# A float32 decoder trunk on one core: how the last SwiGLU's last pair of blocks is turned

## The chip, the core and the metric

The kernel runs on one core of a Trainium2 chip as one launch. The metric is the time of that launch on the device, in microseconds, as the median of several runs. Before the change it is 1646.18 us over three runs, which lie between 1645.61 and 1646.3 us.

Five instruction queues work side by side on the core: PE (matrix products; PEld is its weight load), DVE (vector work), ACT (scalar work and copies), POOL (here mostly an issuer of accumulating DMAs) and SP (an issuer of DMAs). Each works through its own instructions strictly in order, and they wait for each other by semaphores. DMAs are issued from SP, POOL and ACT and are carried out by the core's 16 DMA engines.

## What is computed

Two layers, each a SwiGLU, a mixing block (windowed attention and a short convolution) and a second SwiGLU, then a final norm; one sequence of 512 tokens, width 1024, SwiGLU width 2816, all in float32:

```python
def swiglu(h, w_gate, w_up, w_down):
    return (jax.nn.silu(h @ w_gate) * (h @ w_up)) @ w_down

for l in range(DEPTH):
    x = x + 0.5 * swiglu(rms_norm(x, ffn1_norm[l]), ffn1_wg[l], ffn1_wu[l], ffn1_wd[l])
    ...
    x = x + 0.5 * swiglu(rms_norm(x, ffn2_norm[l]), ffn2_wg[l], ffn2_wu[l], ffn2_wd[l])
return rms_norm(x, final_norm)
```

The change is in the fourth and last SwiGLU, between its up and its down projection.

## The kernel before, in words

**Float32 by parts.** Every float32 operand is split in two parts, a rounded high part (an ACT cast, `wh` for weights) and the rest (a DVE subtraction, `wl`), both at line 223. A product is three matrix multiplications of parts. The weights stream from memory into `raw` buffers (line 206 issues them from SP; line 218 issues from POOL those that are added on top of a loaded buffer), are split, and are used once. Each weight pair is split up to two groups ahead of PE (`SPLIT_AHEAD`), and loaded four groups ahead of that (`LOAD_AHEAD`).

**Seven products for eight.** Large products are done in 2x2 blocks with seven products (`CHAINS`, `SHARES`). The seven steps use the operands b11, b21, t2, t3, t1, t4, b22 of the activations (`Seven.make`, lines 592 to 612, which also splits them) and the forms a11, a12, s2, s3, s1, a22, s4 of the weights. A DVE addition at line 262 or 247 makes s2 in place, and a POOL DMA (line 292 or 285, shown as `raw<-raw`) makes s4.

**The stages of a SwiGLU.** The width of 2816 is 11 blocks of 256. Stage `w` with number b makes blocks b and b+1 of the activations (`winograd2`); its results `ups` are four tiles of 128 tokens x 512 columns. The down projection needs them turned, so that columns lie on partitions. In the last SwiGLU (`LAST`) the pairs 1, 3, 5, 7 and 9 are made one after the other. Then stage `s`, number 1, is the first group of the down projection: it takes the pairs 1 and 3, in seven steps of two halves (`share`, line 836). Stage `e`, number 5, is the last group: it takes the pairs 5, 7 and 9, in seven steps of three parts, two from the pairs 5 and 7 (`ends[0]`) and one from pair 9 (`ends[1]`), and ends with the final norm (`Finale.last`, line 1404).

**Two ways to turn a pair.** (1) By DMA, class `Crossing` for the pairs 1 to 7: ACT lays the 16-bit halves of the float32 words apart (`lay_apart`, line 138), SP issues a DMA transpose, and ACT joins the halves again. Class `Tail` does the same for pair 9 of the inner SwiGLUs (the second and the third), with two DMA transposes for each 128 tokens, one for each half: `during(n)` is called after step n of the first group of the down projection, sends token tiles 0 and 1 at n = 1 and 2 and 3 at n = 2 (line 1190), and joins the first half again at n = 5 (`rejoin`, line 1202). (2) On PE, for pair 9 of the last SwiGLU: `turn` (line 1104) transposes 128x128 squares into PSUM, and ACT copies them out (line 1111). Its four calls stand in `pending`, and `between` of the last SwiGLU's stage `s` flushes two of them after step 1 and two after step 2 of the first group, eight PE transposes each time.

**What sets the order.** The kernel is written as a program of operations; a scheduling layer orders each engine's instructions by its own estimate of when they are ready. `tc.issue_after` forces one order. A buffer's next user waits for the last reader of the one before it. Each DMA also waits until the DMA that took its completion semaphore before it has landed (eight such semaphores are used for those of SP, eight for those of POOL).

Of the kernel before, what the change touches and what calls it, by code (L numbers as in the profile page):

```python
# [8 lines left out]
F32 = mybir.dt.float32  # L9
# [7 lines left out]
P = 128  # L17
D = 1024
S = 512
# [6 lines left out]
NT = S // P  # L26
# [46 lines left out]
def trunk_kernel(  # L73
# [23 lines left out]
    nc = tc.nc  # L97
# [837 lines left out]
    def ffn(norm, stages, after=None, late=None):  # L935

        acts = {}
# [100 lines left out]
        def winograd2(b, between=None):  # L1038


            name = f"{norm.i}_{b}"
            accs = {}
            gates = [g2(f"gate_{name}_{t}") for t in range(NT)]
            ups = [None] * NT
            kept = {}

            hasty = first and b == max(blocks)

            def keep(what, u, src):
                kept[what, u] = g2(f"{what}_{name}_{u}")  # L1050
                nc.scalar.copy(kept[what, u], src)

            for step, (acc, operand, start) in enumerate(CHAINS):
                norm.make(operand)
                xh, xl = norm.forms[operand]
                if start:
                    tag = {"x": "mm", "y": "sc", "w": "aux"}[acc]
                    accs[acc] = [psum(tag, [P, S], f"{acc}_{name}_{u}") for u in range(2)]
                for h in range(2):
                    _, wh, wl = take_split()  # L1060
                    stream(accs[acc], wh, wl, xh, xl, h, start)
                    for u in range(2):
                        out = accs[acc][u]
                        if h == 0:
                            continue
                        if step == 0:
                            keep("p1", u, out)
                        if step == 1:
                            nc.vector.tensor_add(gates[u], out, kept["p1", u])
                            nc.scalar.activation(gates[u], gates[u], AF.Silu)  # L1070
                        if step == 2:
                            keep("u2", u, out)
                        if step == 3:
# [12 lines left out]
                if hasty and step == 5:  # L1086
                    crossing.append(Crossing(b, name, ups, {1: (2, 3)}))
                    for t in range(2):
                        crossing[-1].send(t)
                if not first and step < 3:  # L1090
                    norm.make(CHAINS[step + 4][1])
                if between:
                    between(step)
            if b in blocks and not hasty:
                crossing.append(Crossing(b, name, ups, {0: (0, 1), 1: (2, 3)}))
            if b in blocks:
                return
            if b in tails:
                crossing.append(Tail(b, name, ups))
                return  # L1100
            if b in few:
                raws[b] = [form(f"raw_a{n}_{name}", F32, (P, 2, S)) for n in range(2)]

            def turn(c, tag="sc"):
                tp = psum(tag, [P, S], f"at_{name}_{c}")
                for t in range(NT):
                    nc.tensor.transpose(
                        tp[:, t * P : (t + 1) * P], ups[t][:, c * P : (c + 1) * P], ident
                    )
                if b in few:  # L1110
                    nc.scalar.copy(raws[b][c // 2][:, c % 2, :], tp)
                    return
                if b + c // 2 not in acts:
                    acts[b + c // 2] = [form(f"a{n}_{name}_{c}", shape=(P, 2, S)) for n in "hl"]
                hi, lo = acts[b + c // 2]
                split(hi[:, c % 2, :], lo[:, c % 2, :], tp)

            pending.extend(lambda *tag, c=c: turn(c, *tag) for c in range(NT))

        class Crossing:  # L1120

# [51 lines left out]
        class Tail:  # L1173
# [9 lines left out]
            def during(self, n):  # L1183

                if n == 1:
                    self.to = [form(f"turned{h}_{self.name}", U16, (P, NT, S)) for h in range(2)]
                for t in {1: (0, 1), 2: (2, 3)}.get(n, ()):
                    halves = lay_apart(self.ups[t], f"{self.name}_{t}")
                    for h in range(2):
                        nc.sync.dma_start_transpose(  # L1190
                            self.to[h][:, :, t * P : (t + 1) * P], halves[:, h, :]
                        )
                if n == 5:
                    self.whole = g8(f"raw_a_{self.name}", F32, (P, 2, 2, S))
                    self.rejoin(0)

            def rejoin(self, j):

# [29 lines left out]

        def turns(step):

            if step < 2:
                flush()
            if step == 2:
                flush(2, "mm")
            crossing[:] = [c for c in crossing if not c.step()]

        crossing = []
        sevens = [b for what, b in stages if what == "s"]
        blocks = [b + j for what, b in stages if what in "se" for j in (0, 2)]
        few = [b + 4 for what, b in stages if what == "e"]  # L1240
        tails = [b[0] for what, b in stages if what == "d" and len(b) == 2]
        raws = {}
        pending = []

        def flush(n=1, *tag):
            for _ in range(n):
                if pending:
                    pending.pop(0)(*tag)

        end = None  # L1250
        kept = {}
# [1 line left out]
        for i, (what, b) in enumerate(stages):  # L1253
# [22 lines left out]

# [41 lines left out]
            for c, acc in down(rhs, b == (0,) and not first, final):  # L1318
# [7 lines left out]
                flush()  # L1326
# [435 lines left out]
```

## Time and profile before

| | |
|---|---|
| median of three runs | 1646.18 us (1645.61 to 1646.3) |
| the profiled execution's own time | 1645.93 us |
| its span, first to last instruction | 1644.1 us |
| PE, DVE, ACT, POOL busy | 1633.7, 1376.6, 1107.4, 212.4 us |
| DMA, mean over the span | 186 GB/s |
| first group of the last down projection, on PE | 1539 to 1579 us |
| last group, up to the last product | 1579 to 1638 us |

The profile is one execution. A row of the chain of waits has a start and a length in us and what ran then. A row of instructions in order of time has a start, a length, the engine, the line of the kernel, what is written and read, and in brackets how long the engine was idle before it and what ended that. A row on a tile or a line has the shortest, middle and longest duration in ns. A row of windows has the stretch, then each engine's busy time in it, the granted clock of PE, the mean busy share of the 16 DMA engines (packets that overlap in one engine count twice, so that it can pass 1) and what they moved in GB/s.

### The profile page before, as it was taken

To read this page: it belongs to the slowest core of one execution; us is meant where nothing else is said; L and a number is where in the kernel's file an instruction comes from. 1 tells how busy PE (TensorE), PEld (TensorE's weight loads), DVE (VectorE), ACT (ScalarE), POOL (GpSimd) and SP (SyncE) were. 2 spreads that over 40 slices of the span, in tenths; PEclk is the share of its full clock that TensorE was granted. 3 is DMA by queue.
4 is the path that set the end of the run, shared out by engine and by line. 5 is a ranking of instruction groups with operands and counts; after the bars stand their busy time and mean duration, and the time that the engine had idled before them with its cause. 6 is when DMAs were issued, how large, how long until landed. Compare 5 with 4: busy or idle time off the path is not lost.

```text
span 1644.1 us, 22037 instructions
## 1 busy us (share of the span) xinstructions
PE 1633.7 (99%) x8076; PEld 1380.6 (84%) x8076; DVE 1376.6 (84%) x1812; ACT 1107.4 (67%) x1453; POOL 212.4 (13%) x188
## 2 busy tenths in 40 slices
PE   9999999999999999999999999999999999999998
PEld 7888889988898888888888888888888988888886
DVE  7987779988899977797998777989788998777997
ACT  6447776566567577777765777786565766777665
POOL 0011111100221111111011111110012111111121
PEclk9999999999999999999999999999999999999999
DMA  8379997741397689999866999997125967999992
GB/s 257 86 196 212 220 250 184 173 127 52 103 226 181 181 211 220 217 222 219 220 152 171 226 210 232 206 242 198 52 65 136 229 148 187 222 218 228 248 242 77
DMA packets 277280, 306.10 MB, mean 186 GB/s; under 512 B 93804, under 2 KB 162484, under 8 KB 277172
## 3 DMA queue, kind: packets, MB, share of 16 engines
q1 hardware_dynamic: 236580, 222.24, 46.9%
q0 software_dynamic: 39872, 81.80, 28.9%
q8 instruction: 63, 1.03, 0.2%
q10 hardware_dynamic: 720, 0.66, 0.1%
q14 instruction: 45, 0.37, 0.1%
HBM read 262.71 MB, written 2.10 MB: 161 GB/s over the span
## 4 chain that ended last, share of the span: by engine, by line
PE 94%; DVE 4%; ACT 1%; issue 1%; DMA 0%; SPq 0%; ACTq 0%; DVEq 0%
PE x L827 25%; PE y L827 13%; PE acc L321 8%; PE acc L322 8%; PE acc L324 8%; PE w L827 6%; PE x_s L827 5%; PE x_m L812 3%; PE y_s L827 3%; PE x_s L812 2%; PE w_s L827 2%; PE y_s L812 1%; PE y_m L812 1%; DVE wl L223 1%; PE acc L707 1%; PE x_e L827 1%
## 5 line engine op out<-in xcount | busy, mean ns | idle before, releaser
L223 ACT CAST wh<-raw 128x1024 fp32r<-128x1024 f32 (+1 forms) x491 | 511.1, 1044 | 367.0 <-PE x L827 91.9
L223 DVE TENSOR_TENSOR wl<-raw,wh 128x1024 fp32r<-128x1024 f32 (+1 forms) x491 | 594.6, 1218 | 176.7 <-ACT wh L223 175.6
L321 PE MATMUL acc<-xh,wh 128*128 128x512 f32 x424 | 165.8, 393 | 0.0
L322 PE MATMUL acc<-xl,wh 128*128 128x512 f32 x424 | 165.5, 390 | 0.0
L324 PE MATMUL acc<-xh,wl 128*128 128x512 f32 x416 | 162.3, 390 | 0.0
L218 POOL DMA_DIRECT2D raw<-in_ffn_wu_dram x39 | 48.7, 1248 | 393.9 <-DMA raw<-in_ffn_wu_dram 290.4
L322 PEld LDWEIGHTS acc<-xl,wh 128*128 128x128 f32 x424 | 79.7, 188 | 15.8 <-DVE xl L502 0.2
L321 PEld LDWEIGHTS acc<-xh,wh 128*128 128x128 f32 x424 | 79.8, 188 | 15.7
L324 PEld LDWEIGHTS acc<-xh,wl 128*128 128x128 f32 x416 | 78.1, 188 | 16.3
L218 POOL DMA_DIRECT2D raw<-in_ffn_wg_dram x39 | 48.2, 1262 | 228.5 <-DMA raw<-in_ffn_wu_dram 126.7
L218 POOL DMA_DIRECT2D raw<-in_ffn_wd_dram x34 | 41.0, 1207 | 251.7 <-DVE wl L223 64.1
L262 DVE TENSOR_TENSOR raw<-raw,raw 128x1024 f32<-128x1024 f32 x56 | 68.1, 1220 | 4.7 <-DMA raw<-in_ffn_wu_dram 3.1
L1158 ACT COPY raw_a<-turned 128x1024 uint16<-128x1024 uint16 x48 | 63.1, 1356 | 0.0
L827 PE MATMUL w<-wh,fb21h 128*128 128x512 f32 x152 | 59.2, 390 | 0.0
L827 PE MATMUL w<-wl,fb21h 128*128 128x512 f32 x152 | 59.2, 390 | 0.0
L827 PE MATMUL y<-wh,ft3h 128*128 128x512 f32 x152 | 59.2, 390 | 0.0
L827 PE MATMUL x<-wh,ft2h 128*128 128x512 f32 x152 | 59.2, 390 | 0.0
L827 PE MATMUL x<-wl,ft1h 128*128 128x512 f32 x152 | 59.2, 389 | 0.0
L827 PE MATMUL w<-wh,fb21l 128*128 128x512 f32 x152 | 59.2, 389 | 0.0
L827 PE MATMUL x<-wh,ft1l 128*128 128x512 f32 x152 | 59.2, 389 | 0.0
L827 PE MATMUL x<-wl,ft2h 128*128 128x512 f32 x152 | 59.2, 389 | 0.0
L827 PE MATMUL x<-wl,fb11h 128*128 128x512 f32 x152 | 59.2, 389 | 0.0
(607 smaller groups left out, 4624.3 us busy)
## 6 DMA issues: line engine op xcount, KB each, us to landing
raw<-in_ffn_wu_dram SPq DMA_DIRECT2D x126, 512.0 KB, 5.1
raw<-in_ffn_wd_dram SPq DMA_DIRECT2D x105, 512.0 KB, 5.9
raw<-in_ffn_wg_dram SPq DMA_DIRECT2D x86, 512.0 KB, 5.2
raw<-in_ffn_wu_dram POOLq DMA_DIRECT2D x39, 512.0 KB, 9.0
raw<-in_ffn_wg_dram POOLq DMA_DIRECT2D x39, 512.0 KB, 6.7
raw<-in_w_in_dram SPq DMA_DIRECT2D x36, 512.0 KB, 3.8
raw<-in_ffn_wd_dram POOLq DMA_DIRECT2D x34, 512.0 KB, 9.2
raw<-raw POOLq DMA_DIRECT2D x21, 512.0 KB, 7.0
```

The lines of the kernel that those rows point to most:

```text
L218: nc.gpsimd.dma_start(out=r, in_=rows_of(*more), accum_op=ALU.add)
L223: return nc.scalar.copy(hi, raw), eng.tensor_sub(lo, raw, f32(hi))
L262: nc.vector.tensor_add(a11, a11, s1)
L321: nc.tensor.matmul(acc, hi[:, k, :], rhs[k][0], start=k == first, stop=False)
L322: nc.tensor.matmul(acc, hi[:, k, :], rhs[k][1], start=False, stop=False)
L324: nc.tensor.matmul(acc, lo[:, k, :], rhs[k][0], start=False, stop=k == last)
L707: nc.tensor.matmul(opening[n], (lo if part == "w" else hi)[:, k, :], xl if part == "x" else xh, start=n not in begun, stop=k == KC - 1 and ...
L812: nc.tensor.matmul(accs[c // 2][:, c % 2, :], w[:, k, cols], x_[:, 2 * h + k, :], start=start and c % 2 == 0 and h + k + i == 0, stop=h + ...
L827: nc.tensor.matmul(accs[u], x_[:, 2 * h + k, tok], w[:, k, :], start=start and h + k + i == 0, stop=h + k == 2 and i == 2, skip_group_chec ...
L1158: nc.scalar.copy(words(raws[self.b][:, c, :]), self.to[:, :, c, :])
```

## The change

Pair 9 of the last SwiGLU becomes a `Tail`, as that of the inner ones is. The PE transposes, their PSUM tiles and `pending` with its `flush` go. After step 1 and step 2 of the first group `during` lays the halves apart and issues four DMA transposes each. After step 5 it joins the first half again, as in the inner ones, and after step 6, new and for the last SwiGLU alone, the second. `ends[1]` then reads the joined tile: its operand b11 is made after step 6 instead of step 4, and t2, which was made after step 6, is now made in the last group itself, before its second step. The two 16-bit tiles take two buffers of the pool `xf` in place of the two that held the copies, and the joined tile takes one of the pool `g8`.

```diff
-            if b in blocks:
-                return
             if b in tails:
                 crossing.append(Tail(b, name, ups))
-                return
-            if b in few:
-                raws[b] = [form(f"raw_a{n}_{name}", F32, (P, 2, S)) for n in range(2)]
-
-            def turn(c, tag="sc"):
-                tp = psum(tag, [P, S], f"at_{name}_{c}")
-                for t in range(NT):
-                    nc.tensor.transpose(
-                        tp[:, t * P : (t + 1) * P], ups[t][:, c * P : (c + 1) * P], ident
-                    )
-                if b in few:
-                    nc.scalar.copy(raws[b][c // 2][:, c % 2, :], tp)
-                    return
...
-            pending.extend(lambda *tag, c=c: turn(c, *tag) for c in range(NT))
...
                 if n == 5:
                     self.whole = g8(f"raw_a_{self.name}", F32, (P, 2, 2, S))
+                    raws[self.b] = [self.whole[:, j] for j in range(2)]
                     self.rejoin(0)
+                if n == 6 and after is None:
+                    self.rejoin(1)
...
-            if step < 2:
-                flush()
-            if step == 2:
-                flush(2, "mm")
             crossing[:] = [c for c in crossing if not c.step()]
...
-        few = [b + 4 for what, b in stages if what == "e"]
         tails = [b[0] for what, b in stages if what == "d" and len(b) == 2]
+        tails += [b + 4 for what, b in stages if what == "e"]
...
-                    for n, full in enumerate((lambda b=b: [raws[b + 4], raws[b + 6]], raws[b + 8]))
+                    for n, full in enumerate((lambda b=b: [raws[b + 4], raws[b + 6]], lambda b=b: raws[b + 8]))
                 ]
 
                 def between(step):
-                    if 0 < step < 3:
-                        flush(2, "mm")
-                    for at, n, operand in ((3, 0, "b11"), (4, 1, "b11"), (5, 0, "t2"), (6, 1, "t2")):
+                    for at, n, operand in ((3, 0, "b11"), (5, 0, "t2"), (6, 1, "b11")):
                         if step == at:
                             ends[n].make(operand)
```

As built, the scheduling layer moves these in the last 110 us, and nothing before. PE's order is the same but for the 16 transposes. On SP the eight DMA transposes and the first two loads of the last group come ahead of the two loads of the final norm's gain (line 1409), and these stand just before and just after the first of the two loads of form a22 of the first group; before, the gains came first of all and the loads of a22 stood between those of the last group. On ACT the four copies of line 138 stand around the casts of the first group's forms a12 and s2. On DVE the operands of pair 9 (t2's two subtractions among them) come later, t3 and the sum for t1 of the pairs 5 and 7 move from before to behind the third of the last group's s2 additions, and the low part of the first group's b22 comes one place earlier.

More of the change, by code (lines that the diff above doesn't have):

```diff
@@ L1095, in winograd2 @@
                 crossing.append(Crossing(b, name, ups, {0: (0, 1), 1: (2, 3)}))
-            if b in blocks:
-                return
             if b in tails:
                 crossing.append(Tail(b, name, ups))
-                return
-            if b in few:
-                raws[b] = [form(f"raw_a{n}_{name}", F32, (P, 2, S)) for n in range(2)]
-            def turn(c, tag="sc"):
-                tp = psum(tag, [P, S], f"at_{name}_{c}")
-                for t in range(NT):
-                    nc.tensor.transpose(
-                        tp[:, t * P : (t + 1) * P], ups[t][:, c * P : (c + 1) * P], ident
-                    )
-                if b in few:
-                    nc.scalar.copy(raws[b][c // 2][:, c % 2, :], tp)
-                    return
[L1113 to L1116, printed above, removed]
-            pending.extend(lambda *tag, c=c: turn(c, *tag) for c in range(NT))
         class Crossing:
@@ L1239, in ffn @@
         blocks = [b + j for what, b in stages if what in "se" for j in (0, 2)]
-        few = [b + 4 for what, b in stages if what == "e"]
         tails = [b[0] for what, b in stages if what == "d" and len(b) == 2]
+        tails += [b + 4 for what, b in stages if what == "e"]
         raws = {}
[L1243 to L1248, printed above, removed]
         end = None
@@ L1325, in ffn @@
                 )
-                flush()
                 if final and c == KC // 2:
```

## The prediction

> **What bounds the kernel now.** First the page: is any engine full, and which one carries the chain that ended last?
>
> ```profile
> span 1644.1 us, 22037 instructions
> ...
> PE 1633.7 (99%) x8076; PEld 1380.6 (84%) x8076; DVE 1376.6 (84%) x1812; ACT 1107.4 (67%) x1453; POOL 212.4 (13%) x188
> ...
> PE 94%; DVE 4%; ACT 1%; issue 1%; DMA 0%; SPq 0%; ACTq 0%; DVEq 0%
> ```
>
> PE is full and carries 94% of the chain, so work taken off PE is time, unless another engine then ends the waits. Second, the chain in the place of the change, from the first group of the last down projection into the last group.
>
> ```profile
> 1550.07 0.87 PE at L1107 x8
> ...
> 1556.40 0.87 PE at L1107 x8
> ...
> 1568.17 5.44 PE y_s L827 x24
> ...
> 1576.38 0.80 DVE wl L223
> ...
> 1586.38 0.60 DVE bias L1379
> ...
> 1589.31 4.83 PE x_e L827 x20
> ```
>
> The transposes are two pieces of the chain, 0.87 us each. But from 1576.38 to 1589.31 the chain runs on DVE: PE hardly stands still there, yet DVE is just in time. Third, how full the others are there, DMA in the last two columns.
>
> ```profile
> 1540.00:1544.00 4.00, 4.00 (x19) 3.31 (x18) 3.86 (x5) 2.53 (x4) 2.41 (x2) 1.00 0.57 167
> 1544.00:1556.00 12.00, 12.00 (x58) 10.03 (x57) 9.05 (x10) 6.03 (x7) 1.76 (x2) 1.00 1.08 221
> 1556.00:1570.00 14.00, 14.00 (x67) 11.70 (x66) 13.14 (x16) 12.35 (x13) 4.86 (x4) 1.00 1.02 324
> 1570.00:1594.00 24.00, 23.92 (x105) 19.22 (x105) 24.00 (x27) 13.21 (x14) 4.17 (x4) 1.00 1.09 244
> ```
>
> PE waits 0.08 us in all. DVE has no gap from 1570 to 1594 (24.00 of 24.00), and the DMA engines are full from 1544 to 1594. The change gives PE less and gives ACT, SP and DMA more, just ahead of that stretch.
>
> **What is removed.** Sixteen transposes, 2 x 0.87 = 1.74 us of PE, all on the chain: at most 1.74 us. Four copies on ACT go with them.
>
> ```profile
> L1111 ACT COPY raw_a<-at x4: 579/584/588, 1550.5 to 1557.6; 128x512 f32<-128x512 f32 x4
> ```
>
> **What is added on ACT.** Four copies that lay halves apart and four that join them, whose like are
>
> ```profile
> L138 ACT COPY halves<-u 128x1024 uint16<-128x1024 uint16 x36 | 36.1, 1046 | 0.0
> L1202 ACT COPY raw_a<-turned 128x1024 uint16<-128x1024 uint16 x8 | 10.3, 1357 | 0.0
> ```
>
> That is 4 x 1.05 + 4 x 1.36 - 4 x 0.58 = 7.3 us more on ACT. The first four lie in ACT's idle time: it is busy 2.53 of 4 us up to 1544 and 6.03 of 12 us after, so I cost them at nothing; without that gap they would be 4.2 us. The joining copies stand among the casts of the first group's last forms; ACT has 24 - 13.2 = 10.8 us of idle time in 1570 to 1594, but in pieces, so that DVE must now and then wait for a cast behind a pair of them. I take 0.5 us for this (an estimate, between 0 and one such pair, 2.6 us). The operand b11 of pair 9, made later, is wanted by PE only in the third part of the last group's first step, some 5.4 us after 1578.9, so its delay lies beside the two parts before it.
>
> **What is added and moved on SP.** Eight DMA transposes, two loads of the last group ahead of their place, and two gain loads behind. Before, SP issued the gains early, at 1534.5, and the load of a22's first half (the operand of the step at 1568.17) at 1554.2 (rows below). Now both loads of a22 stand behind all eight transposes. The nearest rows are the inner SwiGLUs' last pair, in the same place:
>
> ```profile
> 733.37 7.92 SPq L1190 DMA_TRANSPOSE turned<-halves  x4
> 748.85 6.52 SPq L1190 DMA_TRANSPOSE turned<-halves  x4
> 1058.01 10.21 SPq L1190 DMA_TRANSPOSE turned<-halves  x4
> 1072.00 6.17 SPq L1190 DMA_TRANSPOSE turned<-halves  x4
> ```
>
> Before, in the place of the change itself, the two gains and the load of a22's first half:
>
> ```profile
> 1534.51 1.38 SPq L1409 DMA_DIRECT2D gain<-in_final_norm_dram  x2
> ```
> ```profile
> 1554.21 0.38 SPq L206 DMA_DIRECT2D raw<-in_ffn_wd_dram  x1
> ```
>
> For a lower bound the transposes of the other pairs, which are twice as large; for landings the loads behind the inner ones' second four, and two `raw<-raw` DMAs each, without transposes beside them and with:
>
> ```profile
> L1134 SPq DMA_TRANSPOSE turned<-halves x64: 1237/1246/2832, 123.3 to 1516.1; - x64
> ```
> ```profile
> L206 SPq DMA_DIRECT2D raw<-in_ffn_wd_dram x3: 420/421/522, 755.5 to 756.6; - x3
> DMA to landing us min/median/max: 5.0/6.9/9.7
> ```
> ```profile
> L292 POOL DMA_DIRECT2D raw<-raw x2: 861/881/901, 1547.6 to 1551.1; - x2
> DMA to landing us min/median/max: 5.5/6.1/6.6
> ```
> ```profile
> L292 POOL DMA_DIRECT2D raw<-raw x2: 861/881/901, 733.5 to 737.3; - x2
> DMA to landing us min/median/max: 5.7/7.9/10.1
> ```
>
> The walk along SP, with the means of the two inner cases. ACT's cast of ft4h_s starts at 1540.44 and takes 1.04 (row below), the first copy 1.05: the first transpose is issued at 1542.5. Four take (7.92 + 10.21) / 2 = 9.1, two loads 0.8, four more (6.52 + 6.17) / 2 = 6.35, then gain, load, gain 1.7: a22's second half is issued at 1560.4, its first half 0.9 before that. (Its buffer must also be free of a `raw<-raw` that starts at about 1550.6 and by the row beside transposes takes 7.9 us: 1558.5, in time.) With the median 6.9 the second half lands at 1567.3. Lower bound: eight at 1.25 give 1542.5 + 10 + 2.5 = 1555.0, but the `raw<-raw` holds it to 1550.6 + 5.5 = 1556.1; with 5.0 it lands at 1561.1. Upper bound: 10.21, 6.52 and 9.7 give 1571.4. I take the middle, since these rows come from the same eight instructions beside the same kinds of transfer.
>
> **Where that meets DVE.** The rows of before around it:
>
> ```profile
> 1540.44 1.04 ACT L223 CAST ft4h_s<-sum_s 128x1024 fp32r<-128x1024 f32 x1
> ...
> 1565.26 1.06 ACT L223 CAST wh<-raw 128x1024 fp32r<-128x1024 f32 x1 [0.49 <-PE x_s L827]
> ```
> ```profile
> 1566.76 1.22 DVE L223 TENSOR_TENSOR wl<-raw,wh 128x1024 fp32r<-128x1024 f32 x1
> ...
> 1582.30 1.22 DVE L223 TENSOR_TENSOR ft3l_e<-raw_a,ft3h_e 128x1024 fp32r<-128x1024 f32 x1
> 1583.43 0.68 DVE L223 TENSOR_TENSOR ft_e<-raw_a,ft_e 128x512 fp32r<-128x512 f32 x1
> ...
> 1586.30 0.68 DVE L1379 SCALAR_TENSOR_TENSOR bias<-x_e,bias 128x512 f32<-128x512 f32 x1
> ```
>
> The cast at 1565.26 is that of a22's second half; its subtraction on DVE starts at 1566.76. From there DVE works without a gap to the addition at 1586.30, which reads PE's sums x_e; PE may add the next step to these sums only after it, at about 1587.0. So DVE needs 1586.98 - 1566.76 = 20.2 us between the two. Behind the change the same stretch lacks ft3l (1.13 from its start to the next) and t3 of pair 9 (0.60, by the chain's row of the addition), and has three small ones more, the low part of b11 and the two subtractions that make t2 of pair 9: 20.2 - 1.13 - 0.60 + 3 x 0.60 = 20.3 us. In the changed kernel the subtraction can start a cast (1.1) after the landing: 1567.3 + 1.1 = 1568.4. PE may then go on at 1568.4 + 20.3 + 0.5 = 1589.2 instead of 1587.0, +2.2 us; PE's wait of 0.08 in the windows falls away with that, and the sum is **+2.1 us**. Everything behind that on PE has the same length as before.
>
> PE itself would come 1.74 us earlier (the step of 1568.17 at 1566.4) and stands still in between: for the first half of a22 (landing about 1566.4, cast and subtraction 2.3, so 1568.7) some 2.3 us, then for DVE the rest, 1.5. The 1.74 us are spent, and 2.1 us more.
>
> Bounds: with the landing at 1561.1 the cast does not wait for it, and PE's gain is the floor, -1.74 us. With 1571.4 it is 1571.4 + 1.1 + 20.3 + 0.5 - 1587.1 = +6.2 us.
>
> [...] The window row has the DMA engines full from 1544 on, and the `raw<-raw` pair takes 6.1 us in the middle without transposes about it and 7.9 us with them. [...]
>
> ```profile
> 738.00:743.00 5.00, 5.00 (x24) 4.14 (x23) 4.52 (x4) 3.94 (x5) 0.11 (x1) 1.00 1.35 145
> ```
>
> Beside the inner transposes the engines moved 145 GB/s at a share of 1.35. [...]
>
> **The rivals.** *A, the full gain.* SP issues the transposes at 1.25 us each in the quieter stretch (share 0.57 up to 1544), a22's second half lands by 1566.76 - 1.74 - 1.1 = 1563.9, and DVE starts its gapless stretch 1.74 us earlier, with PE. For it: the inner twins, beside which PE is busy for 5.00 of 5.00 us (window row above); against it: there the two loads that count were issued ahead of the second four, here behind them, and no inner group of four took under 6.17 us. 1646.2 - 1.74 = 1644.4 us.
>
> *B, slower by more than can be told from no change.* What is moved into the full stretch is eight transposes of 128x512 16-bit words (1.05 MB) and two gains (0.52 MB): at 244 GB/s 6.4 us of the DMA engines. It first meets the last group's loads that POOL adds up, and the latest of them with the least to spare is
>
> ```profile
> L218 POOL DMA_DIRECT2D raw<-in_ffn_wd_dram x1: 1203/1203/1203, 1576.2 to 1576.2; - x1
> DMA to landing us min/median/max: 12.2/12.2/12.2
> ```
> ```profile
> 1591.09 3.04 ACT L223 CAST wh<-raw 128x1024 fp32r<-128x1024 f32 x3 [1.89 <-DVE raw L247]
> ```
>
> landing at 1588.4 for the third of the three casts, at 1593.1: 4.7 us to spare. It decides from a delay of 4.7 us on. 6.4 - 4.7 = 1.7 us on top of 2.1, or the upper bound along SP: +3.8 to +6.2, taken at +5.0: 1651.2 us. For it: the full engines; against it: the casts run ahead of PE, so that part of the delay is hidden.
>
> *C, DVE sets it wholly.* With a landing at 1565.2 the two effects cancel: 1646.2 us. It is the forecast's lower half and not counted apart.
>
> **How the numbers follow.** The profiled execution took 1645.93, 1.83 more than its span; +2.1 gives 1648.0. The median of the runs is 0.25 above it: **1648.3 us**. I give the forecast (from 0 to +3.3 us) 0.44, A and what lies between it and 0 0.19, B 0.35, and 0.02 to more gain than PE alone can give. About 0.2%, 3.3 us, is what a measurement can tell from no change. So within it 0.44 + 0.19 = 0.63; faster by more 0.02; slower by more 0.35. The range reaches down to A, 1644.4, and up into B, 1651.8; the forecast's own is 1646.2 to 1649.5.
>
> **What would show it.** Right: no L1107, the chain's DVE stretch again about 1576 to 1590, now with waits of PE for `wl` in the step y_s at about 1566 and before x_e at about 1588; the two a22 loads issued at 1559 to 1561; DVE without a gap from about 1568. Step by step: each four of the transposes on SP 6 to 10 us (A: 5); `raw<-raw` landing after 8 us; the copies of line 138 done by 1547 without a wait of DVE for them. It would be wrong if a22 landed before 1563.9 (A), if ACT made DVE wait over 2 us behind the joining copies, or if the loads of POOL became the last wait in the last group (B).

## The result, and the profile after

| | median (lowest to highest), us | runs | ratio to before, 95% interval |
|---|---|---|---|
| before | 1645.89 (1645.5 to 1646.3) | 6 | |
| after | 1652.89 (1650.28 to 1655.64) | 6 | 1.0041 (1.0031 to 1.0052) |

The change makes the kernel 7.0 us slower, by more than what can be told from no change (0.2%, 3.3 us). The forecast was 1648.3, the range ended at 1651.8. Before, six runs lie within 0.8 us; after, within 5.4. (Beside later experiments the kernel before itself once spread over 7.6 us, from 1645.79 to 1653.4 in 23 runs, so that a single run says little.) The profiled execution took 1653.55 us, its span is 1651.7, 7.6 longer than before; the ledger below is made against that span. In the changed kernel line 1169 issues the transposes of pair 9 (1190 before), 1378 loads the gains (1409), 1348 adds PE's sums up (1379), 1451 begins the last product (1482); lines 138 to 827 keep their numbers.

The page first: PE has lost its 16 transposes and yet is busy longer (1633.7 us before).

```profile
span 1651.7 us, 22031 instructions
...
PE 1636.2 (99%) x8060; PEld 1380.8 (84%) x8060; DVE 1378.6 (83%) x1812; ACT 1114.1 (67%) x1457; POOL 211.9 (13%) x188
```

The same windows as before the change, and two later ones (columns: PE, PEld, DVE, ACT, POOL, granted clock, DMA share, GB/s).

```profile
1544.00:1556.00 12.00, 12.00 (x54) 9.69 (x53) 10.40 (x11) 7.64 (x9) 2.55 (x3) 1.00 1.12 196
1556.00:1570.00 14.00, 11.99 (x51) 9.38 (x50) 6.97 (x8) 6.26 (x6) 0.00 (x0) 0.98 1.15 281
1570.00:1594.00 24.00, 21.79 (x89) 17.38 (x89) 22.54 (x26) 18.77 (x19) 8.62 (x8) 0.93 1.10 289
...
1592.00:1602.00 10.00, 9.81 (x36) 8.02 (x37) 8.64 (x10) 3.67 (x4) 0.86 (x1) 0.83 1.08 213
1626.00:1634.00 8.00, 8.00 (x37) 6.62 (x36) 8.00 (x10) 4.39 (x7) 3.69 (x2) 1.00 0.01 2
```

Three things show. Between 1556 and 1570, DVE does 6.97 us of work where it did 13.14, and POOL none: they wait for data. PE stands still 2.0 us in that window and 2.2 in the next. And the granted clock, 1.00 in every window shown of before, falls to 0.93 and 0.83. The list of PE's waits from 1540 on names what it waited for:

```profile
PE x_e L827 <- DVE bias L1348: 2.2, 1, 2.2
PE y_s L827 <- ACT wh L223: 1.5, 1, 1.5
PE y_s L827 <- DVE wl L223: 0.5, 1, 0.5
PE x_e L1451 <- DVE wl L223: 0.4, 1, 0.4
```

The waits for `wh` and `wl` in y_s are those for the load of form a22. SP's instructions in order of time lead to it, and the row of POOL's two `raw<-raw` in the same stretch:

```profile
1542.62 7.68 SPq L1169 DMA_TRANSPOSE turned<-halves  x4
1550.39 2.58 SPq L206 DMA_DIRECT2D raw<-in_ffn_wd_dram  x2
1553.06 8.50 SPq L1169 DMA_TRANSPOSE turned<-halves  x4
1561.66 0.53 SPq L1378 DMA_DIRECT2D gain<-in_final_norm_dram  x1
1562.30 0.37 SPq L206 DMA_DIRECT2D raw<-in_ffn_wd_dram  x1
1562.76 1.25 SPq L1378 DMA_DIRECT2D gain<-in_final_norm_dram  x1
1564.12 3.06 SPq L206 DMA_DIRECT2D raw<-in_ffn_wd_dram  x6
```
```profile
L292 POOL DMA_DIRECT2D raw<-raw x2: 861/881/901, 1547.7 to 1551.3; - x2
...
DMA to landing us min/median/max: 8.3/8.6/8.9
```

a22's first half is issued at 1562.30, its second at 1564.12. Where they landed is seen on ACT, whose casts wait for them, and then on DVE:

```profile
1567.15 1.04 ACT L223 CAST wh<-raw 128x1024 fp32r<-128x1024 f32 x1 [5.21 <-DMA raw<-in_ffn_wd_dram]
1570.27 1.04 ACT L223 CAST wh<-raw 128x1024 fp32r<-128x1024 f32 x1 [2.08 <-DMA raw<-in_ffn_wd_dram]
```
```profile
1568.22 1.23 DVE L223 TENSOR_TENSOR wl<-raw,wh 128x1024 fp32r<-128x1024 f32 x1 [6.17 <-ACT wh L223]
1571.35 1.23 DVE L223 TENSOR_TENSOR wl<-raw,wh 128x1024 fp32r<-128x1024 f32 x1 [1.90 <-ACT wh L223]
...
1591.36 0.68 DVE L1348 SCALAR_TENSOR_TENSOR bias<-x_e,bias 128x512 f32<-128x512 f32 x1
...
1594.90 1.22 DVE L223 TENSOR_TENSOR ft3l_e<-raw_a,ft3h_e 128x1024 fp32r<-128x1024 f32 x1
1596.04 0.68 DVE L223 TENSOR_TENSOR ft_e<-raw_a,ft_e 128x512 fp32r<-128x512 f32 x1
```

DVE has no gap (no brackets) from 1571.35 to the addition that ends at 1592.04. On PE the step behind it shows its wait, and in the same rows the clock:

```profile
1592.19 0.47 PE L827 MATMUL x_e<-wh,ft2h_e 128*128 128x512 f32 x1 [2.21 <-DVE bias L1348]
...
1592.96 0.40 PE L827 MATMUL x_e<-wh,ft2h_e 128*128 128x512 f32 x1
1593.19 0.48 PE L827 MATMUL x_e<-wh,ft2l_e 128*128 128x512 f32 x1
1593.47 0.63 PE L827 MATMUL x_e<-wl,ft2h_e 128*128 128x512 f32 x1
```

Matmuls that began 0.23 us apart and took 0.40 take 0.63 from 1593.47 on, and then begin 0.43 apart, for 3.3 us. The granted clock from 1593 to 1597 is 0.57; behind the waits in y_s, from 1570 to 1573, it is 0.52.

**The ledger.** PE is ahead of before at first: its step x_s(t1) starts at 1561.16 instead of 1562.57. Then DVE's subtraction of a22's second half starts 4.59 us later (1571.35 instead of 1566.76), and DVE's stretch from there to the end of the addition is 20.69 long instead of 20.22: +0.47. That is +5.06, and x_e(t2) starts at 1592.19 instead of 1587.13: +5.06 too. The slow matmuls add 1.22 (that step lasts 9.87 instead of 8.65): line 1451 begins at 1634.70 instead of 1628.42, +6.28. From there to the end are 17.0 us instead of 15.7: +1.3. Together 4.59 + 0.47 + 1.22 + 1.3 = 7.6.

### The profile page after: what moved, and what is told of

It is laid out like the page before. It is cut to its first block, busy times and chain, and to the rows that moved or that the text cites. A ratio compares the mean times of both kernels' runs of the same rounds, so it can differ in the third digit from the quotient of the medians.

```text
span 1651.7 us, 22031 instructions
## 1 busy us (share of the span) xinstructions
PE 1636.2 (99%) x8060; PEld 1380.8 (84%) x8060; DVE 1378.6 (83%) x1812; ACT 1114.1 (67%) x1457; POOL 211.9 (13%) x188
## 4 chain that ended last, share of the span: by engine, by line
PE 93%; DVE 3%; ACT 2%; DMA 1%; issue 1%; SPq 0%; ACTq 0%; DVEq 0%
PE x L827 25%; PE y L827 13%; PE acc L321 8%; PE acc L322 8%; PE acc L324 8%; PE w L827 6%; PE x_s L827 5%; PE x_m L812 3%; PE x_s L812 2%; PE y_s L827 2%; PE w_s L827 2%; PE y_s L812 1%; PE y_m L812 1%; DVE wl L223 1%; PE x_e L827 1%; PE acc L707 1%
## 5 line engine op out<-in xcount | busy, mean ns | idle before, releaser
L321 PEld LDWEIGHTS acc<-xh,wh 128*128 128x128 f32 x424 | 79.8, 188 | 15.7
L827 PE MATMUL x<-wh,ft1h 128*128 128x512 f32 x152 | 59.1, 389 | 0.0
L827 PE MATMUL x<-wh,ft2l 128*128 128x512 f32 x152 | 59.1, 389 | 0.0
```

Of the source, the lines that this page charges most:

```text
L321: nc.tensor.matmul(acc, hi[:, k, :], rhs[k][0], start=k == first, stop=False)
L827: nc.tensor.matmul(accs[u], x_[:, 2 * h + k, tok], w[:, k, :], start=start and h + k + i == 0, stop=h + k == 2 and i == 2, skip_group_chec ...
```

## The experiments

The theory that the result left standing (theory 1): a22 is late by its place on SP, behind eight transposes. Against it stood that it is the traffic: the transposes load the DMA engines, so that whatever is in flight with them lands late, and the place matters little. Beside these, the clock and DVE's last stretch had to be sized.

| kernel | median, us | before beside it | ratio, 95% interval | span |
|---|---|---|---|---|
| second_behind | 1651.87 | 1646.20 | 1.0033 (1.0020 to 1.0045) | 1651.2 |
| all_behind | 1650.95 | 1646.20 | 1.0031 (1.0019 to 1.0043) | 1648.2 |
| keep_busy | 1651.96 | 1646.20 | 1.0038 (1.0025 to 1.0052) | 1648.8 |
| plain_1k | 1649.36 | 1646.90 | 1.0013 (1.0004 to 1.0023) | 1649.7 |
| no_traffic | 1646.82 | 1646.90 | 1.0002 (0.9990 to 1.0013) | 1644.1 |
| before_plus | 1653.54 | 1646.90 | 1.0034 (1.0022 to 1.0047) | 1650.8 |
| no_traffic_early | 1648.92 | 1645.98 | 1.0018 (1.0009 to 1.0027) | 1647.3 |
| dve_add_second | 1646.07 | 1645.98 | 1.0000 (0.9991 to 1.0009) | 1644.0 |
| dve_add | 1647.01 | 1646.25 | 1.0003 (0.9994 to 1.0012) | 1645.7 |
| before_dve | 1646.43 | 1646.25 | 1.0000 (0.9991 to 1.0008) | 1646.1 |
| dve_relief | 1645.10 | 1646.39 | 0.9993 (0.9985 to 1.0002) | 1642.6 |
| before_relief | 1646.00 | 1646.39 | 0.9996 (0.9987 to 1.0005) | 1646.3 |

### a22 ahead of the transposes: second_behind and all_behind

The sends are held behind the second load of a22, whose instruction the load helper keeps; at n == 2 in the one kernel, at both steps (n > 0) in the other.

```diff
-        nc.sync.dma_start(r[:, a:b, :], rows_of(src, k0 + a, b - a, col, wide))
+        state["load", n] = nc.sync.dma_start(r[:, a:b, :], rows_of(src, k0 + a, b - a, col, wide))
...
+                        with tc.issue_after(state["load", min(roomy) - 1].ins) if after is None and n == 2 else nullcontext():
...
```

> The changed kernel with one thing moved: the second four transposes of pair 9 stand behind the last load of a22 on SP's queue; every other engine's order, every instruction and every byte is the same. Theory 1 (the place on SP sets the end): in the changed kernel's profile a22's second half was issued at 1564.1 and landed at 1570.2; here SP is held only by the raw<-raw landings (1556.0 and 1560.2), so it is issued at about 1560.3 and lands at about 1566; DVE's stretch of 20.7 us then ends at about 1588.0 instead of 1592.0, PE's waits are short and both stretches at half clock go: 1652.9 - 4.0 - 1.2 = about 1647.7 (1646 to 1649). Theory 2 (the transposes' bytes fill the DMA engines wherever they stand): loads land as late as before within 1 us, 1651 or more. Theory 3 (the four joining copies on ACT): they stay where they were, so 1652.9.

> All eight transposes behind the last load of a22 on SP's queue. Theory 1: raw<-raw meets no transposes and lands as in the kernel before (1554.2 and 1556.7), a22's loads are issued right after and land at 1558.6 and 1561.2, so DVE's stretch can start with PE, 1.7 us earlier than before: that alone gives 1644.4. But the transposes are then issued from about 1557 to 1574 and land near 1578, while ACT's first joining copy stands at about 1574 and holds the casts behind it 3 to 5 us: 1646 to 1650, taken at 1648. Theory 2: the bytes come 10 us later into the loads of the last group and hold those: 1651 or more, with waits of PE for loads of the last group.

In second_behind SP stood ready for a22 behind the first four transposes, but could not issue it. Its rows, and that of `raw<-raw`:

```profile
1542.83 8.46 SPq L1171 DMA_TRANSPOSE turned<-halves  x4
...
1552.85 0.93 SPq L1378 DMA_DIRECT2D gain<-in_final_norm_dram  x2
1558.91 4.41 SPq L206 DMA_DIRECT2D raw<-in_ffn_wd_dram  x2
1563.37 5.96 SPq L1171 DMA_TRANSPOSE turned<-halves  x4
```
```profile
DMA to landing us min/median/max: 10.9/11.1/11.4
```

SP is free at 1553.8 and issues at 1558.91: a22 is loaded into the buffer that `raw<-raw` reads, and of the two the first took 10.9 us and the second 11.4 (5.5 to 6.6 before the change). The chain of waits shows the two behind one another:

```profile
1547.96 10.90 DMA raw<-raw
...
1558.91 9.11 DMA raw<-in_ffn_wd_dram
...
1576.53 12.52 DMA raw<-in_ffn_wd_dram
```

So theory 1 fell as the whole cause: a22's second half landed at 1569.29 instead of 1570.17, and the time is 4.2 us above the 1647.7 that it gave. There are two gates, SP's place and the buffer that `raw<-raw` holds. In the changed kernel SP was the later one (`raw<-raw` had landed at 1556.0 and 1560.2, and SP came to a22 at 1562.30 and 1564.12); with SP's place moved, it was the buffer.

In all_behind (1651.0, where theory 1 gave 1648) both gates opened: with hardly a transpose beside it `raw<-raw` took 4.7 and 5.7 us, a22 was issued from 1552.99, landed 1558.3 and 1559.7, and PE did not wait in y_s at all. But SP then reached the last group's loads, the first two excepted, only at 1566.77, and POOL, which adds to them, its first at 1571.55 (1563.12 before). The new last wait stands in its chain:

```profile
1567.91 6.94 DMA raw<-in_ffn_wd_dram
...
1575.45 9.37 DMA raw<-in_ffn_wd_dram
...
1584.85 1.23 DVE raw L247
...
1587.42 9.91 PE x_e L827 x36
```

This is the place of rival B. x_e(t2) begins 0.3 us later than before the change, and the clock behind its wait of 2.3 us (granted 0.68 from 1587.4 to 1592.4) and a longer end make it 4.1 of span. In each of the three places on SP that were tried with `raw<-raw` as DMAs, something lands late.

### PE kept busy through its waits: keep_busy

Empty matmuls (of zeros) stand ahead of the two steps that wait: 7 before y_s(t4), 10 before x_e(t2).

```diff
+                if isinstance(y, Finale) and (step, h) == (5, 0): [nc.tensor.matmul(accs["y"][0], zero[:, :P], zero, start=False, stop=False, skip_group_check=True) for _ in range(7)]
...
+                if step == 1: room = [[psum("sc", [P, S], f"y_e_{u}") for u in range(2)]]; spin(10, room[0][0])
```

> The changed kernel with 17 empty matmuls of 128x512 bf16 on PE (7 ahead of the first group's step y_s with t4, 10 ahead of the last group's step x_e with t2), where PE waited 1.5 and 2.2 us; nothing is taken away, but ACT's and DVE's order in the last 40 us is another one. If a wait of PE makes the granted clock fall to half for the next 3.3 us (the profile of the changed kernel: matmuls 430 ns apart from 1569.5 to 1572.7 and from 1593.5 to 1596.7, else 227), then here no matmul stands 430 ns apart, the step x_e with t2 takes 8.2 us instead of 9.9, and the time is 1.2 to 1.7 us less: about 1651.5. If the clock has another cause, the slow stretches stay and the time is 1652.9 or more.

The window over the step x_e(t2), against the 0.83 of after:

```profile
1591.60:1600.40 8.80, 8.63 (x37) 6.88 (x38) 8.80 (x10) 4.22 (x5) 0.86 (x1) 1.00 1.07 209
```

The clock stays at 1.00 and the step takes 8.65 us instead of 9.87, as before the change: the 1.22 us are the clock's. The median is only 0.9 below that of after, and the intervals overlap, so that the gain in time isn't shown. The scheduling layer also put DVE's and ACT's work of the last 40 us in another order here, which confounds the span.

### The traffic itself: plain_1k, no_traffic and before_plus

plain_1k sends the same bytes at the same places without transposing (pair 9 isn't turned); no_traffic leaves the transposes out and clears their targets on POOL instead; before_plus is the kernel before with copies and eight transposes into tiles that nobody reads.

```diff
+                        to, rows = self.to[h][:, :, t * P : (t + 1) * P], self.to[h][:, t]
+                        if after is None: nc.sync.dma_start(rows, halves[:, h, :])
+                        else: nc.sync.dma_start_transpose(to, halves[:, h, :])
...
```
```diff
+                        if after is None: (t == 0 and nc.gpsimd.memset(self.to[h], 0)); continue
```
```diff
+                        for t in (2 * step - 2, 2 * step - 1):
+                            halves = lay_apart(kept_ups[-1][t], f"spare_{t}")
+                            for h in range(2):
+                                nc.sync.dma_start_transpose(spare[h][:, :, t * P : (t + 1) * P], halves[:, h, :])
```

> The changed kernel with each of pair 9's eight DMA transposes in the last SwiGLU replaced by a plain DMA of the same 128 KB (rows of 1 KB) in the same place of SP's queue; all engines' orders are the same, and pair 9 is not turned, so its products are left wrong. New theory (from the run with the second four behind, where raw<-raw took 10.9 and 11.4 us beside the transposes and a22 landed at 1569.3 though SP was free): transposing is what crowds the DMA engines, in small packets, and holds up raw<-raw and the loads. Then plain copies cost little: raw<-raw lands within 8 us, a22's second half by 1563, and PE's 1.7 us come back as far as DVE lets them: 1644.5 to 1646.5. Rival 1, the bytes count: 1.05 MB more take as long plain, a22 lands at 1568 or later, 1650 or more. Rival 2, ACT's joining copies and DVE's order set the end: 1649 or more with a22 landing early.

> The changed kernel with the eight transposes of the last SwiGLU left out (their targets are cleared by two memsets on POOL, so pair 9's part of the product is left out); the eight copies on ACT, the order of ACT, DVE and PE stay. If the DMA traffic is the whole cost: a22 lands at about 1559 and 1562 as before, DVE can start its stretch when PE frees the buffer, about 1765.3 - 200 = 1565.1, and ends it 20.7 us later at 1585.8; PE, 1.7 us earlier, waits for it 0.4 us: 1644.4 to 1645.5. If the copies on ACT or the later making of pair 9's operands cost something of their own, it shows here alone: every us over 1645.5 is theirs.

> The other way round: the kernel before, with its PE transposes kept, and beside them the same four copies that lay halves apart and the same eight DMA transposes, whose result nobody reads (on SP they stand among the loads, the last four behind a22's). If the traffic is the cost, raw<-raw takes 9 to 11 us instead of 6, a22's second half lands at 1566 or later, POOL's loads of the last group come 4 us or more later, and the time is 1648 to 1653 although PE, the joining copies and the operands are those of before. If the cost lies in the joining copies or in where pair 9's operands are made, the time stays at 1646.2 within 1 us.

(The second of these has a slip: 1765.3 - 200 is 1565.3 and not 1565.1; 0.2 us changes nothing here.) Without the traffic the whole loss is gone: 1.0002. With the bytes alone it is 1.0013, with the transposes 1.0041. So by the medians about 2.5 us go with the bytes (1649.4 against 1646.8), and 3.5 more with their being transposed. plain_1k ran beside other runs of before than after did; by the ratios the two parts are 0.11% and 0.28%. The intervals of plain_1k and no_traffic overlap, so that the bytes' part isn't clear of the noise; those of plain_1k and after don't.

plain_1k also missed its forecast (1644.5 to 1646.5, with `raw<-raw` landing within 8 us), and its rows of SP and of `raw<-raw` say why:

```profile
1548.62 3.85 SPq L1170 DMA_DIRECT2D turned<-halves  x4
...
1559.51 0.37 SPq L206 DMA_DIRECT2D raw<-in_ffn_wd_dram  x1
```
```profile
DMA to landing us min/median/max: 10.0/10.3/10.6
```

The second four plain copies hold SP for 3.85 us where the transposes hold it for 8.50. But `raw<-raw` took 10.6 and 10.0 us beside them, longer than beside the transposes (8.3 and 8.9), SP issued nothing from 1553.37 until the first of them had landed at 1559.5, and DVE's subtraction of a22's second half started only at 1569.43. So plain copies save SP's time and not that of `raw<-raw`: it isn't transposing as such that makes `raw<-raw` slow.

no_traffic (forecast 1644.4 to 1645.5) shows something else: it is not faster than before either, though PE has the 1.74 us less. Its list of PE's waits, and PE's first instruction of line 1451 in order of time:

```profile
PE x_e L827 <- DVE bias L1348: 1.1, 1, 1.1
PE x_e L1451 <- DVE wl L223: 0.4, 1, 0.4
```
```profile
1627.17 0.39 PE L1451 MATMUL x_e<-wh,fb22h_e 128*128 128x512 f32 x1
```

PE reaches line 1451 at 1627.17, 1.25 ahead of before, and both spans are 1644.1: the last stretch has grown by as much. before_plus, meant as the clean price of the traffic in the old kernel, took 1653.5, but one of ACT's casts stood still for 5.75 us there (up to 1568.91; SP was on the last four of the unread transposes until 1567.18), so it gives no clean price. The profile shows nothing that the cast waited for; a buffer, since the targets of the unread transposes come from the same pool, is a guess.

### The operands made earlier: no_traffic_early

no_traffic with the halves joined two steps and one step earlier, and pair 9's operands made at the steps of the kernel before.

```diff
-                if n == 5:
+                if n == (3 if after is None else 5):
...
-                if n == 6 and after is None:
+                if n == 5 and after is None:
...
-                    for at, n, operand in ((3, 0, "b11"), (5, 0, "t2"), (6, 1, "b11")):
+                    for at, n, operand in ((3, 0, "b11"), (4, 1, "b11"), (5, 0, "t2"), (6, 1, "t2")):
```

> As the run without the transposes (1646.8, ratio 1.000 to before, though its PE lacks 1.74 us of transposes), but with the joining copies at steps 3 and 5 and pair 9's operands made at steps 4 and 6, as in the kernel before (pair 9's part of the product is left out again). In that run PE was 1.25 us ahead of before up to the last step, and the end came at the same 1644.1: the last 17 us took 1.25 us more. If this is so because DVE makes pair 9's t2 and t3 and ft3l later and runs behind to the end, it goes here: 1645.0 to 1645.8. If DVE's whole load sets the end whatever the order, it stays at 1646.8, within 0.7.

Its ratio is 1.0018 where no_traffic has 1.0002 (the ends of the two intervals overlap by a little), and the forecast gain did not come. ACT's joins now stand ahead of casts that DVE waits for (3.23 us before the subtraction at 1565.29), PE waits 3.25 before x_e(t2), and the clock falls behind that (granted 0.89 from 1585 to 1600). So late joins are the better choice here: these earlier ones found no room on ACT.

### The other DMA taken away: dve_add_second, dve_add and before_dve

The two `raw<-raw` of the last stage s become additions on DVE, which has the room for them there (busy 10.40 of 12 us from 1544 to 1556 in the changed kernel, 11.93 in dve_add). That takes away both the buffer's wait and a traffic of SBUF to SBUF; the transposes stay. dve_add_second has SP's order of second_behind besides. dve_add has that of the change, except that a22's first half stands ahead of the eighth transpose and both gains ahead of the second half. before_dve is the kernel before with this edit alone.

```diff
-                if what == "s3" and how == "share":
+                if what == "s3" and how == "share" and u != min(roomy) - 10:
                     nc.gpsimd.dma_start(out=a12, in_=a11, accum_op=ALU.add)
                 elif what == "s3":
                     nc.vector.tensor_add(a12, a12, a11)
```

> The run with the second four transposes behind a22's loads, and in it the two raw<-raw of the last s stage (512 KB each, SBUF to SBUF, adding) made by two additions on DVE instead of two DMAs: the result is the same, the DMA engines lose as many bytes as the transposes bring (1.05 MB), and a22's buffers come free at 1552 instead of 1559 and 1563. DVE pays 2 x 1.14 us ahead of its stretch. If the meeting of transposes and raw<-raw is what makes a22 late, its loads are issued by 1555 and land by 1563, PE does not wait in the step y_s with t4, and the time is 1646.5 to 1648.5. If the transposes hold up whatever loads there are, a22 lands at 1566 or later: 1650 or more.

> The changed kernel with the two raw<-raw of the last s stage made on DVE, and the transposes left in their place, ahead of a22's loads on SP (a22's first half now stands between the seventh and the eighth, the second behind them). With both moved the time was 1646.1, with the SP order moved alone 1651.9. If the meeting of transposes and raw<-raw is the cost, this alone gives most of it back: SP issues the second four without long stops, a22's second half goes out at about 1559 and lands by 1565, 1646 to 1648. If the place on SP matters as much, a22 lands at 1567 or later: 1649 to 1651.

> The control: the kernel before with the two raw<-raw of the last s stage made on DVE, PE's transposes kept. In its profile a22's halves landed at 1558.6 and 1561.2 and the second half's cast waited until 1565.3 for PE, so raw<-raw is not waited for: the time stays at 1646.0 within 0.8, and what DVE's additions gave back in the changed kernel is the transposes' cost. If the additions on DVE are a gain of their own, this kernel takes 1644.5 or less, and the transposes still cost 1.5 us or more in the kernel with both moved.

| ratio to before | `raw<-raw` by DMA | added up on DVE |
|---|---|---|
| PE transposes | 1 | 1.0000 (0.9991 to 1.0008) |
| DMA transposes | 1.0041 (1.0031 to 1.0052) | 1.0003 (0.9994 to 1.0012) |

Neither alone costs anything that can be measured; together they cost 0.4%. It is the meeting of the eight transposes with the two accumulating DMAs that makes the loss. The edit takes away both the buffer that these hold and the traffic that they make. In the changed kernel the buffer was free before SP came to a22, as said, and in no_traffic `raw<-raw` took 9.3 and 8.2 us, held a22 until 1559, and nothing was lost; so there it is SP's time on the transposes that counts. The rows of SP in dve_add show it: a22 is issued at 1556.22 and 1559.19.

```profile
1552.32 3.81 SPq L1169 DMA_TRANSPOSE turned<-halves  x3
1556.22 0.53 SPq L206 DMA_DIRECT2D raw<-in_ffn_wd_dram  x1
1556.80 1.20 SPq L1169 DMA_TRANSPOSE turned<-halves  x1
...
1559.19 6.02 SPq L206 DMA_DIRECT2D raw<-in_ffn_wd_dram  x7
```

The second four transposes take 5.0 us here and 8.5 in the changed kernel: 3.5 of the 4.9 us by which a22's second half is issued earlier. `raw<-raw` isn't all that slows them: the first four take 7.6 here too, and the second four, behind a22's loads, 7.2 in dve_add_second and 6.5 in dve_relief. In dve_add_second PE waits nowhere in y_s, is 1.35 us ahead at line 1451 and ends with before to 0.1 us, like no_traffic.

### DVE relieved: dve_relief and before_relief

dve_add_second without the sums for t1 and t4 of pair 9 (two times 0.6 us of DVE in the last group; the operands are then other numbers), and the same in the kernel before.

```diff
-                    if what == "t1":
+                    if what == "t1" and kc != 2:
...
-                    if what == "t4":
+                    if what == "t4" and kc != 2:
```

> The kernel with the second four behind a22's loads and raw<-raw on DVE (1646.1), and in it two small DVE operations of the last group left out, the sums that make t1 and t4 of pair 9 (0.6 us each), so that pair 9's products are left wrong there. In that kernel PE stands 1.25 us ahead of before at its last step and the end is the same. If DVE, full from 1602 to 1626 (8.00 of 8), holds PE's gain back, 1.2 us less of it gives 0.8 to 1.3 us: 1644.8 to 1645.3. If PE's gain is lost elsewhere, 1646.1 within 0.4.

> The control: the kernel before with the same two sums of pair 9 left out. Its DVE has idle time in the last group (6.56 of 8 us busy from 1620 to 1628) and PE has none, so less DVE work gives nothing: 1646.0 within 0.5. If it falls by 0.8 or more, DVE held back the kernel before as well.

The wait of line 1451 is gone from dve_relief, and from there to the end are 1642.6 - 1626.79 = 15.8 us, as in before (15.7) and before_relief (15.8); in no_traffic, dve_add and dve_add_second they are 16.9 to 17.0. (In keep_busy and no_traffic_early, with other orders on DVE, they are 15.8.) In time it is 1.3 us under before, with an interval that includes none, and before_relief is 0.4 under, so it fits that DVE keeps PE's gain from the end, and isn't shown by the times.

## Why the prediction was wrong

**What was right.** The mechanism: a22 late behind the transposes, PE waiting for it in y_s, then DVE's gapless stretch deciding, PE waiting 2.2 us before x_e. The first transpose was forecast at 1542.5 and issued at 1542.62; the copies of line 138 were done by 1546.4 in ACT's idle time, without a wait of DVE (row `1544.39 1.99` of ACT's order of time); `raw<-raw` was forecast at 7.9 us and took 8.3 and 8.9; DVE's stretch with the 0.5 for ACT's joins was forecast at 20.8 and took 20.69; b11's delay cost nothing.

```profile
1544.39 1.99 ACT L138 COPY halves<-p 128x1024 uint16<-128x1024 uint16 x2
```

**The term that was mis-sized: a22's landing.** "With the median 6.9 the second half lands at 1567.3"; it landed at 1570.17, +2.9, inside the bound of 1571.4 that stood beside it (by luck: the issue at 1564.12 lies beyond the 1561.7 in that bound, and only the load was quicker than its 9.7), and that is nearly all of the difference between +2.1 and +5.06 at x_e(t2). The latency was even shorter, 6.05. What was longer was the walk on SP: the second four transposes 8.50 instead of 6.35, the two loads between 2.58 instead of 0.8, gain, load, gain 2.35 instead of 1.7, less 1.4 for the first four (7.68 instead of 9.1). The rows of the inner cases had been taken as "the same eight instructions beside the same kinds of transfer". They aren't: the inner `raw<-raw` start at 733.53 and 1058.17, beside the first fours (7.92 and 10.21), and have landed before the second fours (6.52 and 6.17). Here the second four stand beside `raw<-raw`; without it the same four took 5.0 (dve_add). What a transpose costs SP differs with what it meets, and the walk took each four by its number and not by what is in flight.

**The step that failed: "Everything behind that on PE has the same length as before."** It cost 2.5 us of the 7.6, in two parts. One is the clock: behind two waits of about 2 us (1.49 and 0.53 in y_s, 2.21 before x_e) the granted clock was 0.52 and 0.57 for some 3 us each. The first such stretch, in y_s, lay beside DVE's work and cost nothing; the second made the step x_e(t2) 1.22 longer, and keep_busy, where the clock stayed at 1.00, has that step at its old length. The other is DVE: the forecast took `ft3l` (1.13) and t3 (0.60) out of DVE's stretch, but they aren't removed, they are moved. In the rows above they stand at 1594.90 and 1596.04, behind the addition. There DVE has hardly any room: it is busy 8.00 of the 8 us up to 1634, where it was busy 6.56 in the window that answers to it:

```profile
1620.00:1628.00 8.00, 8.00 (x37) 6.59 (x36) 6.56 (x9) 4.39 (x7) 4.22 (x2) 1.00 0.00 0
```

So PE waits for it once more at line 1451, and the end comes 1.3 later. That the same 1.2 to 1.3 stand in no_traffic, dve_add and dve_add_second, and not in dve_relief, fits it. Both parts rest on the profiles: the times of keep_busy and dve_relief move the right way, but not clear of the noise.

**Rival A, the full gain, was not missed by bad luck.** With no transpose traffic at all (no_traffic), and this order of DVE's work, the 1.74 us of PE don't reach the end: A would be 0.9989 of before, and the interval is 0.9990 to 1.0013. **Rival B's time (1651.2) was nearest,** by the part of its price that went along SP, and in part by luck, since the 2.5 us of clock and end stood in none of its terms; its other part, the POOL loads as the last wait, is seen in all_behind and in second_behind's chain (1576.53 12.52), and in the changed kernel DVE is without a gap there. POOL's first load is 9.0 us later (1572.11 instead of 1563.12), and that is hidden.

**Transposes against plain copies.** In this place the eight transposes were not as fast as plain copies of the same bytes: with the copies (plain_1k) the time was 1649.4, with the transposes 1652.9, and the second four held SP for 3.85 and for 8.50 us.

## What to carry to other kernels

Price a transpose that is moved to the DMA engines by what is in flight in the same microseconds and by which buffers that other transfer holds, not by the engine time that it takes off (1.74 us of PE here, against second fours that held SP for 5.0 us without `raw<-raw` and 8.50 beside it), and take the upper end where the place is a new one. Ask first whether the engine next in line could use the gain: here DVE was full late in the last group (23.96 of 24 us from 1602 to 1626 in no_traffic), and 1.74 us off PE were worth nothing even where the turning cost nothing (1.0002). And what leaves an engine's critical stretch by being moved must be paid for where it goes.

## What the runs showed of the hardware that was not expected

**Two accumulating DMAs and eight transposes cost together what neither costs alone,** 0.4% by the table above. It shows on SP: the second four transposes take 8.50 us beside `raw<-raw` (8.69 in keep_busy) and 5.0 without it in dve_add. How long `raw<-raw` itself takes (512 KB, SBUF to SBUF) tells less. With no DMA of pair 9 beside it, it took 5.5 and 6.6 us before the change and 8.2 and 9.3 in no_traffic; with hardly a transpose beside it 4.7 and 5.7 (all_behind); with transposes 8.3 and 8.9 in the change, 10.9 and 11.4 in second_behind; beside plain copies 10.0 and 10.6. The engines counted as full in the longest of these, at a low rate; a window of second_behind in which the two are in flight with what is left of the first transposes, two loads and the gains:

```profile
1555.70:1561.00 5.30, 5.30 (x25) 4.39 (x24) 5.03 (x7) 4.38 (x5) 0.00 (x0) 1.00 1.06 134
```

Why a transpose holds SP longer than a copy was not tried further.

**Behind most waits of about 2 us the clock fell to about half** (granted 0.52 and 0.57 in after). Waits of 2.2, 2.3 and 3.25 us before x_e(t2) (after, plain_1k, second_behind, all_behind, no_traffic_early), and those of 1.49 and 0.53 in y_s of after and of 2.98 and 0.71 in y_s of before_plus, were each followed by matmuls 0.43 us apart for 3.0 to 3.4 us; waits of 1.06 to 1.4 (dve_add_second, no_traffic, dve_add, before_plus) were not (granted 1.00 behind the 1.3 of dve_add), and neither was one of 2.2 and 0.5 in y_s of second_behind:

```profile
1566.70:1576.20 9.50, 6.74 (x29) 5.06 (x28) 6.90 (x7) 7.85 (x8) 0.97 (x1) 1.00 1.10 253
```

So the length of the wait alone doesn't decide; what else does wasn't shown. Whether after's wide spread of 5.4 us comes of runs with none, one or two such stretches wasn't tried.
